# Three chunks of a hybrid layer's q/k/v projection, by seven products of half blocks and ahead of the cache decode instead of beside it

## The chip, the core and the metric

One core of one Trainium2 chip runs the whole kernel. The metric is device time in microseconds (us). Before the change it is 1711.08 us, the median of 3 runs (1709.94 to 1711.53). Engines are named as the profile names them: PE (TensorE, matmuls), PEld (its weight loads), DVE (VectorE), ACT (ScalarE), POOL (GpSimd), SP (SyncE, which issues the DMAs).

## What is computed

One layer over 1024 prompt tokens and 128 sample tokens (8 sequences of 16). Its first part is what matters here: a norm, one projection to q, k and v for two groups of 8 heads, and two kinds of attention. The sample tokens also attend to a cache (1024 past frames in group A, 512 in group B).

```python
h = rmsnorm(x, g_mix)
q_a, k_a, v_a, q_b, k_b, v_b = split_heads(h, w_in)      # h @ w_in, 1024 x 3072
...
def stick_breaking(q, k, v, q_pos, k_pos):               # group A
    z = jnp.einsum('bqhd,bkhd->bhqk', q, k).astype(jnp.float32) * (HEAD_DIM ** -0.5)
    causal = k_pos[None, :] < q_pos[:, None]
    log_keep = jnp.where(causal, jax.nn.log_sigmoid(-z), 0.0)
    between = lax.cumsum(log_keep, axis=3, reverse=True) - log_keep
    w = jnp.where(causal, jnp.exp(jax.nn.log_sigmoid(z) + between), 0.0)
    return jnp.einsum('bhqk,bkhd->bqhd', w.astype(v.dtype), v)
...
x = x + mix @ w_out
h = rmsnorm(x, g_ffn)
x = x + (jax.nn.silu(h @ w_gate) * (h @ w_up)) @ w_down
```

## The kernel before

Tokens lie in nine tiles of 128: tiles 0 to 7 are the prompt, tile 8 (`NP`) the sample tokens. Every fp32 operand of a large product is split into a high part (a cast on ACT) and a low part (a subtraction, `sub`, L104), and `mm3` (L99 to L102) issues three matmuls for each pair: high by high, high by low, low by high.

`qkv` (L227) makes the projection in twelve chunks of 256 columns, named (group, w, c): group 0 is A and 1 is B, w is 0 for queries, 1 for keys, 2 for values, c is the half. It is a generator: each `yield` is one step of the *main* work, and other generators are advanced between its steps.
- A step of `others` (keys and values, L258) is one token tile: 24 matmuls with 256 moving columns. Three tiles on, keys are turned by PE transposes (L273) and stored; values are split and stored.
- A step of `queries` (L244) is one half of the chunk's columns by three token tiles: 24 matmuls with 384 moving columns, then a scaled split (`parts`) and two stores.

`load` brings a chunk's weights (1 MB) and splits them, one chunk ahead; there is one buffer for raw weights and two for split ones.

The order of the main work is the list `loads` (L299): keys of A, queries of A, values of A, keys, values, queries of B. The stage ahead of the decode runs 36 steps of it (L785 to L795): A's keys (18), A's queries (12), and tile 8's share of A's values (6). Then `decode(0, ...)` (L334, group A's sample tokens against the cache) runs beside 30 steps: `advance(project, dec, R2, 30)` (L806) takes R2 = 1.2 decode steps for each main step. PE's order is as written there (`manual_schedule`). A decode step transposes a block of cached keys on PE (L405), copies it out on ACT and DVE (L406), multiplies (L427), takes sigmoids, and for an earlier block turns weights (L414) and multiplies by cached values (L468). Once a sequence DVE scans the kept shares and multiplies them in (`between`, L114, and L444).

Then the attention over the prompt (`attention`, L515, run from L817) takes 1.95 of its units for each remaining main step (values and queries of B, 30 steps). A unit is one head by one tile of 128 queries: two score matmuls for each block of keys (L579, L580), two sigmoids on ACT (L582, L583), the scan on DVE (`between`, L111 and L114), a multiplication on POOL (L592), and five units later (`LAG`) the transposes (L610), their split on ACT and DVE (L614, L105), and the products with the values (L633, L634). A head has 8 units and 36 transposes at L610; group A has 8 heads, so 64 units. Outside `manual_schedule` a scheduler with its own model of durations sets the order on each engine. After group A's heads, group B's heads run beside `decode(1, ...)`.

The feed-forward part already multiplies by seven products of half blocks instead of eight (`product`, L1077; `sums`, L1099).

## Time and profile before

| | |
|---|---|
| median of 3 runs | 1711.08 us |
| profiled execution, its own time | 1711.13 us |
| span of that execution, first to last instruction | 1709.3 us |
| granted clock of TensorE, mean | 0.989 |
| PE, DVE, ACT, POOL busy | 1654.1, 1080.7, 813.3, 832.5 us |
| first instruction of the cache decode (L405) | 151.75 us |
| first scores of the attention (L579) | 333.64 us |

The time of an execution is 1.8 us more than its span. Matmuls overlap: the profile gives one with 256 moving columns as 0.28 us long, but the next one starts 0.12 us later. What one costs in a stream is therefore read from start to start, and "busy" on PE is no measure of free room.

### The profile page before, as it was taken

Reading aid. Unit: us, or ns where it says so; the run is one execution under the profiler, and the core shown is the slowest. Engines: PE = TensorE matmul, PEld = TensorE weight load, DVE = VectorE, ACT = ScalarE, POOL = GpSimd, SP = SyncE. Lnnn points to the kernel's source line nnn. Section 1 sums busy time; section 2 is a strip of 40 time slices with the busy share of each in tenths; the row PEclk is TensorE's granted clock in tenths of the full one; section 3 lists DMA queues with packets and bytes.
Section 4 is the critical chain, followed back from the end, with each engine's and each line's share of the span. In section 5 each row is a group of like instructions: output and inputs, shape, how many; then the busy total and the mean of one; then the engine's idle time right before and its main releaser. Section 6 shows DMA issues by size and latency. Waiting matters only on the chain.

```text
span 1709.3 us, 27802 instructions
## 1 busy us (share of the span) xinstructions
PE 1654.1 (97%) x10308; PEld 1422.4 (83%) x10308; DVE 1080.7 (63%) x1725; ACT 813.3 (48%) x1724; POOL 832.5 (49%) x675
## 2 busy tenths in 40 slices
PE   8999999999998999798999999999999999999998
PEld 7998888989996778787878888888888878788887
DVE  6111444369789766754677566666655497798875
ACT  5323545367768767643663333333333244433673
POOL 2313311278466412222565555555555378958763
PEclk9999999999998999899999999999999999999999
DMA  5846898666469985856422222222222697722222
GB/s 193 276 151 217 268 294 291 185 186 184 114 186 268 278 269 159 244 160 198 144 91 96 96 96 95 96 95 96 87 86 87 226 377 252 248 70 112 98 99 99
DMA packets 172810, 293.50 MB, mean 172 GB/s; under 512 B 16641, under 2 KB 96257, under 8 KB 170370
## 3 DMA queue, kind: packets, MB, share of 16 engines
q1 hardware_dynamic: 172674, 291.71, 52.4%
q8 instruction: 82, 1.34, 0.3%
q14 instruction: 54, 0.44, 0.1%
HBM read 204.77 MB, written 86.90 MB: 171 GB/s over the span
## 4 chain that ended last, share of the span: by engine, by line
PE 76%; DMA 6%; DVE 6%; POOL 4%; ACT 4%; issue 4%; SPq 1%; POOLq 0%; DVEq 0%; ACTq 0%
PE ps L1081 25%; PE ps L100 6%; PE ps L101 6%; PE ps L102 6%; PE pt L1081 4%; PE pt L610 3%; PE pt L405 2%; PE pt L1352 2%; PE ps L1352 2%; PE po L634 2%; PE acc L468 2%; DMA v<-sv 2%; PE po L633 1%; PE sdec L427 1%; PE S L579 1%
## 5 line engine op out<-in xcount | busy, mean ns | idle before, releaser
L105 POOL TENSOR_TENSOR wlo<-wraw,whi 128x512 fp32r<-128x512 f32 (+1 forms) x121 | 217.6, 1821 | 125.2 <-ACT whi L159 121.7
L100 PE MATMUL ps<-whi,hTh 128*128 128x256 f32 x576 | 168.7, 293 | 1.3 <-ACT st L267 1.3
L101 PE MATMUL ps<-wlo,hTh 128*128 128x256 f32 x576 | 164.7, 286 | 0.0
L102 PE MATMUL ps<-whi,hTl 128*128 128x256 f32 x576 | 164.5, 286 | 0.0
L159 ACT CAST whi<-wraw 128x512 fp32r<-128x512 f32 (+1 forms) x118 | 86.2, 746 | 75.5 <-PE ps L1081 27.4
L100 PEld LDWEIGHTS ps<-whi,hTh 128*128 128x128 f32 x576 | 111.3, 193 | 8.0 <-issue 6.0
L101 PEld LDWEIGHTS ps<-wlo,hTh 128*128 128x128 f32 x576 | 111.4, 193 | 0.2
L102 PEld LDWEIGHTS ps<-whi,hTl 128*128 128x128 f32 x576 | 111.1, 193 | 0.6 <-DVE hTl L105 0.2
L592 POOL TENSOR_TENSOR w<-w,keep 128x127 f32<-128x127 f32 (+4 forms) x64 | 82.3, 1291 | 57.1 <-DVE keep L114 35.1
L105 DVE TENSOR_TENSOR wtl<-pt,wth 128x512 fp32r<-128x512 f32 (+1 forms) x192 | 93.9, 511 | 14.9 <-ACT wth L614 14.6
L614 ACT CAST wth<-pt 128x512 fp32r<-128x512 f32 (+1 forms) x192 | 85.6, 468 | 35.5 <-PE pt L610 34.9
L610 PE MATMUL pt<-ident,w 128*128 128x128 f32 x528 | 90.2, 285 | 11.7 <-DVE osb L649 4.1
L114 DVE TENSOR_TENSOR_SCAN keep<-keep,zero 128x128 f32<-128x128 f32 (+7 forms) x64 | 99.4, 1556 | 1.5
L610 PEld LDWEIGHTS pt<-ident,w 128*128 128x128 f32 x528 | 63.9, 144 | 25.1 <-issue 7.0
L579 PE MATMUL S<-qk 128*128 128x384 f32 (+2 forms) x192 | 73.2, 383 | 6.2 <-ACT keep L583 3.8
L633 PE MATMUL po<-wth,vk 128*128 128x256 f32 (+1 forms) x304 | 76.4, 283 | 0.8 <-DMA vk<-v 0.5
L105 POOL TENSOR_TENSOR actl<-actr,acth 128x1024 fp32r<-128x1024 f32 (+1 forms) x22 | 60.5, 2751 | 33.0 <-DMA sr<-acts 20.7
L634 PE MATMUL po<-wtl,vk 128*128 128x256 f32 (+1 forms) x304 | 72.8, 284 | 0.0
L101 PE MATMUL ps<-hTl,whi 128*128 128x384 f32 x192 | 65.6, 342 | 0.0
L406 DVE COPY kT<-pt 128x512 f32<-128x512 f32 x48 | 33.0, 687 | 51.6 <-PE pt L405 47.6
L100 PE MATMUL ps<-hTh,whi 128*128 128x384 f32 x192 | 65.5, 341 | 0.0
L102 PE MATMUL ps<-hTh,wlo 128*128 128x384 f32 x192 | 64.9, 338 | 0.0
(450 smaller groups left out, 5304.8 us busy)
## 6 DMA issues: line engine op xcount, KB each, us to landing
draw<-in_cache_sb_k SPq DMA_DIRECT2D x32, 512.0 KB, 5.7
draw<-in_cache_sb_v SPq DMA_DIRECT2D x32, 512.0 KB, 5.3
act<-sg SPq DMA_DIRECT2D x11, 1152.0 KB
actr<-act SPq DMA_DIRECT2D x22, 576.0 KB, 6.3
wraw<-in_w_in SPq DMA_DIRECT2D x11, 1024.0 KB, 9.3
wraw<-in_w_gate SPq DMA_DIRECT2D x11, 1024.0 KB, 5.4
wraw<-in_w_up SPq DMA_DIRECT2D x11, 1024.0 KB, 5.4
v<-sv SPq DMA_DIRECT2D x36, 256.0 KB, 4.6
```

Of the source, the lines that this page charges most:

```text
L100: T.matmul(out, lhsT=ah, rhs=bh, start=start, stop=False)
L101: T.matmul(out, lhsT=ah, rhs=bl, start=False, stop=False)
L102: T.matmul(out, lhsT=al, rhs=bh, start=False, stop=stop)
L105: return eng.tensor_tensor(out, a, hi.bitcast(F32), op=ALU.subtract)
L114: V.tensor_tensor_scan(rev, rev, zero[:, 0:1].to_broadcast([P, n - d]), keep[:, n - d : n - d + 1], op0=ALU.mult, op1=ALU.max)
L159: A.copy(h[:, o], v[:, o])
L579: T.matmul(sc, lhsT=hd["qq"][:, qs], rhs=hd["kkh"][:, kc], start=True, stop=False)
L610: T.transpose(pt[:, (c - c0) * P : (c - c0 + 1) * P], w[:, c * P : (c + 1) * P], ident)
L614: A.copy(wth[:, ks, qs], pv)
L633: T.matmul(dst, lhsT=vs, rhs=wth[:, kb - base, c0:c1], start=(i == 0), stop=False)
L634: T.matmul(dst, lhsT=vs, rhs=wtl[:, kb - base, c0:c1], start=False, stop=(i == nkb - 1))
L1081: T.matmul(out, lhsT=a[x][:, k], rhs=b[y][:, k], start=(not more and k == 0 and n == 0), stop=(k == 3 and n == 2), skip_group_check=more)
```

## The change

Three of the twelve chunks, A's second query chunk (0, 0, 1) and B's two key chunks (1, 1, 0) and (1, 1, 1), are made by `seven`. The prompt is cut into two halves of four tiles, the 1024 inputs into two halves, the 256 columns into two halves; seven block products of 12 matmuls with 512 moving columns (`product`) take the place of eight. They need sums of blocks: `sum_forms` builds four sums of input blocks once (14 DVE instructions on 128x512 for each of four k, and 4 casts on ACT), beside the steps of the second key chunk and the first query chunk; `weight_sums` builds four of the weights for each chunk (4 DVE instructions, then 4 casts on ACT and 4 subtractions on POOL). Tile 8 is done apart (`sampled`): 48 matmuls with 128 moving columns for the query chunk, 24 with 256 for a key chunk.

The token groups become 4, 4 and 1 tiles, so that a step of `queries` has 512 moving columns, or 128 for tile 8. The order of the main work becomes: A's keys, A's first query chunk, the three chunks by `seven`, tile 8's share of A's values, and only then the decode; the rest of the values goes beside the decode (23 steps, 1.5 decode steps each), and the last six steps of values and all of B's queries beside the attention (2.25 units each). Pools for the sums are opened after the first nine steps and closed just ahead of the decode.

```diff
-        def __init__(self):
+        def __init__(self, ends=(3, 6, 9)):
...
-            g, o = divmod(t, 3)
+            g, o = self.group(t)
...
+    def weight_sums(pool, v):
+
+        (a11, a12), (a21, a22) = [[v[:, k * 4 : k * 4 + 4, f * P : (f + 1) * P] for k in range(2)] for f in range(2)]
+        s1, s2, s3, s4 = [pool.tile([P, 4, P], F32, name=f"s{i}", tag=f"s{i}", bufs=1) for i in (1, 2, 3, 4)]
+        V.tensor_tensor(s1, a21, a22, op=ALU.add)
+        V.tensor_tensor(s2, s1, a11, op=ALU.subtract)
+        V.tensor_tensor(s3, a11, a21, op=ALU.subtract)
+        V.tensor_tensor(s4, a12, s2, op=ALU.subtract)
+        return s1, s2, s3, s4
...
+        def queries(grp, c, wts, gs=(0, 2, 1)):
...
-            order = [(pr, g) for pr in range(2) for g in range(3)]
-            if (grp, c) == (1, 1):
-                order.sort(key=lambda x: x[1])
+            order = [(pr, g) for g in gs for pr in range(2)]
             for pr, g in order:
                 m = slice(pr * P, (pr + 1) * P)
-                ps_ = ps["o"].tile([P, 384], F32, name="ps", tag="O")
+                n = hT.count[g] * P
+                ps_ = ps["o"].tile([P, 512], F32, name="ps", tag="O")[:, :n]
...
+                    if k == 3 and n > 256:
+                        yield
+                cut = min(n, stg[1])
+                cut = 256 if cut == 384 else cut
+                for o in range(0, n, cut):
+                    d = min(cut, n - o)
+                    transposed_out(grp, 0, c * 2 + pr, hT.first[g] * P + o, d, parts(d, ps_[:, o : o + d], (1 - 2 * grp) * HD**-0.5))
                 yield
...
+        def sum_forms():
...
+            for k in range(4):
...
+                yield op(t1, q0h, p0h, minus)
+                yield op(t1, t1, q0l, ALU.add)
+                yield op(t1, t1, p0l, minus)
+                hi("T1", t1)
+                yield op(t2, q1h, t1, minus)
+                yield op(t2, t2, q1l, ALU.add)
+                hi("T2", t2)
+                yield lo("T1", t1)
+                yield op(t4, p1h, t2, minus)
+                yield op(t4, t4, p1l, ALU.add)
+                hi("T4", t4)
+                yield lo("T2", t2)
+                yield op(t3, q1h, q0h, minus)
+                yield op(t3, t3, q1l, ALU.add)
+                yield op(t3, t3, q0l, minus)
+                hi("T3", t3)
+                yield lo("T4", t4)
+                yield lo("T3", t3)
...
+        def sampled(grp, w, c, wts):
...
+                for pr in range(2):
+                    ps_ = ps["o"].tile([P, 512], F32, name="ps", tag="O")[:, :P]
+                    m = slice(pr * P, (pr + 1) * P)
+                    for k in range(KT):
+                        mm3(ps_, wts[0][:, k, m], wts[1][:, k, m], *hT.tok(NP, k), k == 0, k == KT - 1)
+                    transposed_out(grp, 0, c * 2 + pr, NP * P, P, parts(P, ps_, (1 - 2 * grp) * HD**-0.5))
+                return
+            ps_ = ps["o"].tile([P, 256], F32, name="ps", tag="O")
+            for k in range(KT):
+                mm3(ps_, *hT.tok(NP, k), wts[0][:, k], wts[1][:, k], k == 0, k == KT - 1)
+            st = stg[0].tile([P, 3, 256], F32, name="st", tag="st", bufs=2)
+            A.copy(st[:, 0], ps_)
+            rows_of(grp, c, st, NP, 1)
...
+        def seven(grp, w, c, nxt, summed):
+
...
+            S = {1: weight_sum_parts(pool_, 1, s)}
+            B11, B21, B22 = hT.block(0, 0), hT.block(0, 1), hT.block(1, 1)
...
+            a = bank()
+            product(a, quarter(wts, 0, 0), B11)
+            u2 = pool_.tile([P, 512], F32, name="u2", tag="u2", bufs=2)
+            u3 = pool_.tile([P, 512], F32, name="u3", tag="u3", bufs=1)
+            A.copy(u2, a)
...
+            fetch(*nxt)
+            yield
+            product(a, quarter(wts, 1, 0), B21, True)
+            S[3] = weight_sum_parts(pool_, 3, s)
+            yield
+            done(0, 0, a)
+            b = bank()
+            product(b, S[1], F["T2"])
+            V.tensor_tensor(u2, u2, b, op=ALU.add)
+            yield
+            cc = bank()
+            product(cc, S[2], F["T3"])
+            V.tensor_tensor(u3, u2, cc, op=ALU.add)
+            load(*nxt, summed)
+            yield
+            d = bank()
+            product(d, S[0], F["T1"])
+            V.tensor_tensor(u3, u3, d, op=ALU.add)
+            yield
+            sampled(grp, w, c, wts)
+            done(1, 1, u3)
+            yield
+            product(cc, quarter(wts, 1, 1), F["T4"], True)
+            V.tensor_tensor(u3, u2, cc, op=ALU.add)
+            done(1, 0, u3)
+            yield
+            product(d, S[3], B22, True)
+            V.tensor_tensor(u2, u2, d, op=ALU.add)
+            done(0, 1, u2)
+            yield
+
...
+        wide["open"]()
+        sums_ = sum_forms()
+        load(0, 0, 0)
...
+        yield from beside(others(0, 1, 1, ready[0, 1, 1], range(3)))
+        load(0, 0, 1, True)
+        yield from beside(queries(0, 0, ready[0, 0, 0]))
+        for _ in sums_:
+            pass
+        chunks = [(0, 0, 1), (1, 1, 0), (1, 1, 1)]
+        for i, x in enumerate(chunks):
+            after = chunks[i + 1] if i + 1 < len(chunks) else None
+            yield from seven(*x, after or (0, 2, 0), after is not None)
+        fetch(0, 2, 1)
+        load(0, 2, 1)
+        yield from others(0, 2, 0, ready[0, 2, 0], (2,))
+        yield from others(0, 2, 1, ready[0, 2, 1], (2,))
+        wide["close"]()
+        yield from others(0, 2, 1, ready[0, 2, 1], (0, 1))
+        ch.turn = 1 - ch.turn
+        load(1, 2, 0)
+        yield from others(0, 2, 0, ready[0, 2, 0], (0, 1))
+        load(1, 2, 1)
+        yield from others(1, 2, 0, ready[1, 2, 0], range(3))
+        load(1, 0, 0)
+        yield from others(1, 2, 1, ready[1, 2, 1], range(3))
+        load(1, 0, 1)
+        yield from queries(1, 0, ready[1, 0, 0])
+        yield from queries(1, 1, ready[1, 0, 1])
...
+        sv = dk.tile([P, 2, 4, 2, HD], F32R, name="sv")
+        odd = dk.tile([P, 2], F32, name="odd")
+        place = dk.tile([P, 528 if grp else 16], F32, name="bias" if grp else "own_place")
+        loaded = {(x, w): dk.tile([P, 4, P], F32, name=f"s{w}{x}", tag=f"s{w}", bufs=1) for w in "qk" for x in (0,)}
         for i in range(ahead):
             fetch(i)
...
-    stg = pool(right, "stg", "right", 2)
+    sstack = ExitStack()
+    stg = [pool(sstack, "stg", "right", 2), 512]
...
+    hT = Transposed((4, 8, 9))
+    for g in (0, 2, 1):
...
+    def open_wide():
+        fp = pool(wstack, "qforms", "left")
+        wide["forms"] = {n: [fp.tile([P, KT // 2, 512], F32R, name=n + x) for x in "hl"] for n in ("T1", "T2", "T4", "T3")}
+        wide["pool"] = pool(wstack, "qsums", "left")
+        wide["banks"] = wstack.enter_context(tc.tile_pool(name="ps_w", bufs=3, space=PSUM, side="right", reuse_waits="tile"))
...
+    def close_wide():
+        wstack.close()
+        sstack.close()
+        stg[:] = pool(right, "stg2", "right", 2), 384
+        wide["closed"] = True
...
-    advance(project, None, 0, 36 - (NT - 1))
+    while "closed" not in wide:
+        next(project)
...
-        advance(project, dec, R2, 30)
+        advance(project, dec, 1.5, 24 - 1)
...
-    advance(project, att, 1.95)
+    advance(project, att, 2.25)
```

Counted over PE's whole order, the matmuls of the projection stand so (transposes: those of keys):

| stage on PE | 256 wide | 384 wide | 512 wide | 128 wide | transposes |
|---|---|---|---|---|---|
| before: up to the first L405 | 624 | 288 | 0 | 0 | 36 |
| before: from there to the first scores | 799 | 0 | 0 | 0 | 36 |
| before: from there on | 305 | 288 | 0 | 0 | 0 |
| after: up to the decode's first transpose | 696 | 0 | 348 | 96 | 56 |
| after: from there to the first scores | 648 | 0 | 9 | 0 | 0 |
| after: from there on | 0 | 0 | 183 | 96 | 0 |

The first place is on PE ahead of the decode, where A's second query chunk is made; `hTh_140` holds the second half of the inputs of the first tiles, `whi` and `wlo` are the weights. Before it reads:

```order
L100 MATMUL ps<-hTh_140,whi 128x384
L101 MATMUL ps<-hTl_141,whi 128x384
L102 MATMUL ps<-hTh_140,wlo 128x384
L100 MATMUL ps<-hTh_140,whi 128x384
L101 MATMUL ps<-hTl_141,whi 128x384
```

With the change, `T3` and `T1` being sums of inputs and `S2` and `S0` sums of weights:

```order
L216 MATMUL ps<-hTh_140,whi 128x512
L216 MATMUL ps<-hTl_141,whi 128x512
L216 MATMUL ps<-hTh_140,wlo 128x512
L216 MATMUL ps<-T3l,S2h 128x512
L216 MATMUL ps<-T3h,S2l 128x512
L216 MATMUL ps<-T1h,S0h 128x512
L216 MATMUL ps<-T1l,S0h 128x512
```

The products are wider, and some of them read tiles that DVE, ACT and POOL have just made. The second place is on DVE in the same stage. Before, it holds the splits of the keys (`sq<-pt`) and of the queries (`sq<-ps`), and copies of values:

```order
L105 TENSOR_TENSOR sq<-pt,sq 128x384 x4
L267 COPY st<-ps 128x256
L105 TENSOR_TENSOR sq<-pt,sq 128x384 x2
L237 SCALAR_TENSOR_TENSOR sq<-ps,sq 128x384 x12
L267 COPY st<-ps 128x256 x3
```

With the change (L368 are sums of inputs in scratch tiles `tS..`, L228 to L231 sums of weights):

```order
L105 TENSOR_TENSOR T2l<-tS3l,T2h 128x512
L368 TENSOR_TENSOR tS0l<-tS0l,hTl_149 128x512
L368 TENSOR_TENSOR tS0h<-tS0h,hTl_141 128x512
L368 TENSOR_TENSOR tS3h<-tS3h,hTl_139 128x512
L368 TENSOR_TENSOR tS0l<-tS0l,hTl_147 128x512
L368 TENSOR_TENSOR tS3l<-hTh_148,tS3h 128x512
L105 TENSOR_TENSOR T4l<-tS0h,T4h 128x512
L105 TENSOR_TENSOR T1l<-tS3h,T1h 128x512
```

Between two splits of keys or queries now stand up to fourteen instructions with two inputs in SBUF. The third place is on PE in the attention, in the fifth head, which before has main matmuls (L100 to L102) between its own:

```order
L634 MATMUL po<-wtl,vk 128x256
L633 MATMUL po<-wth,vk 128x128
L634 MATMUL po<-wtl,vk 128x128
L610 MATMUL pt<-ident,w 128x128 x4
L100 MATMUL ps<-hTh_142,whi 128x384
L579 MATMUL S<-qk 128x384
L580 MATMUL S<-qk 128x384
L101 MATMUL ps<-hTl_143,whi 128x384
```

With the change (L771 and L772 are the scores, L802 the transposes, L825 and L826 the products with values):

```order
L802 MATMUL pt<-ident,w 128x128 x4
L771 MATMUL S<-qk 128x512
L772 MATMUL S<-qk 128x512
L802 MATMUL pt<-ident,w 128x128
L771 MATMUL S<-qk 128x384
L772 MATMUL S<-qk 128x384
L771 MATMUL S<-qk 128x512
L772 MATMUL S<-qk 128x512
L802 MATMUL pt<-ident,w 128x128 x6
```

From the fourth head's end on, no main matmul stands in PE's order: the main matmuls between the last transposes of successive heads were 185, 98, 80, 75, 78, 75, 2 and 0 before, and are 105, 67, 81, 26, 0, 0, 0 and 0 now.

171 lines of the change are left out of this document (100 added, 71 removed).

## The prediction

> **What bounds the kernel now.** I read the page first, then a table of windows by stage, then PE's timeline for start-to-start times, then the chain of waits and the costliest groups of single stages. The page says that PE is busy nearly all the time:
>
> ```profile
> span 1709.3 us, 27802 instructions
> PE   8999999999998999798999999999999999999998
> DVE  6111444369789766754677566666655497798875
> ```
>
> That is not yet a bound, since overlapping matmuls count in full. The windows below are cut at the first cache transpose (151.75), the first scores (333.64), and then at the last transpose of each head of group A's attention (each 36th at L610):
>
> ```profile
> core 0: us, PE busy (x) PEld busy (x) DVE busy (x) ACT busy (x) POOL busy (x), PEclk, DMA share, GB/s
> 50.00:151.75 101.75, 100.46 (x711) 100.22 (x710) 12.95 (x25) 25.04 (x50) 26.67 (x17) 1.00 0.62 205
> 151.75:333.64 181.89, 178.85 (x1998) 158.29 (x1996) 74.43 (x120) 83.14 (x218) 35.84 (x42) 0.99 0.80 257
> 333.64:372.55 38.91, 35.77 (x264) 33.75 (x265) 21.73 (x28) 21.93 (x57) 26.30 (x31) 0.96 0.80 225
> 372.55:400.09 27.54, 26.53 (x209) 25.23 (x208) 24.72 (x35) 20.20 (x55) 20.88 (x24) 1.00 0.55 156
> 400.09:427.33 27.24, 26.84 (x191) 25.65 (x190) 25.34 (x36) 19.98 (x49) 23.76 (x25) 1.00 0.60 185
> 427.33:454.13 26.80, 26.80 (x186) 26.07 (x184) 22.94 (x38) 19.09 (x46) 15.45 (x20) 1.00 0.51 141
> 454.13:481.59 27.46, 27.46 (x189) 26.66 (x188) 22.28 (x35) 19.10 (x46) 14.11 (x18) 1.00 0.47 137
> 481.59:508.38 26.79, 26.79 (x185) 26.02 (x184) 21.46 (x34) 17.54 (x45) 14.03 (x19) 1.00 0.52 151
> 508.38:530.91 22.53, 17.46 (x110) 14.22 (x109) 21.71 (x30) 17.61 (x45) 15.33 (x21) 0.87 0.99 297
> 530.91:563.06 32.15, 28.65 (x248) 22.94 (x247) 29.70 (x59) 28.20 (x72) 21.50 (x25) 0.93 0.92 255
> ```
>
> Three stages, three states. Ahead of the decode (first row) PE is full and DVE nearly idle, 13 of 102 us. Beside the decode PE is full and the DMA is at 0.80. In the attention the middle heads have PE full with DVE at 80% and more; the seventh head (508 to 531), beside which no main matmul is left, takes 22.53 us, and there DVE is the full one: 21.71 us. So a head costs about 22.5 us by DVE, whatever PE has to do, and main work beside it is free up to the difference.
>
> What a matmul costs from start to start, by width:
>
> ```profile
> 28.07 0.28 PE L102 MATMUL ps<-whi,hTl 128*128 128x256 f32 x1
> 28.19 0.28 PE L100 MATMUL ps<-whi,hTh 128*128 128x256 f32 x1
> ...
> 103.96 0.34 PE L101 MATMUL ps<-hTl,whi 128*128 128x384 f32 x1
> 104.13 0.33 PE L102 MATMUL ps<-hTh,wlo 128*128 128x384 f32 x1
> ...
> 902.20 0.39 PE L1081 MATMUL ps<-B21h,whi 128*128 128x512 f32 x1
> 902.43 0.39 PE L1081 MATMUL ps<-B21l,whi 128*128 128x512 f32 x1
> ...
> 362.26 0.28 PE L579 MATMUL S<-qk 128*128 128x128 f32 x1
> 362.37 0.27 PE L580 MATMUL S<-qk 128*128 128x128 f32 x1
> 362.48 0.27 PE L634 MATMUL po<-wtl,vk 128*128 128x128 f32 x1
> ```
>
> So 256 columns cost 0.120 us, 384 cost 0.173, 512 cost 0.227, and 128 cost 0.11: nearly as much as 256, where 0.06 would be in proportion. From the chain of waits, in the decode:
>
> ```profile
> 200.10 0.31 PE ps L100
> 203.16 0.87 PE pt L405 x8
> 205.48 1.02 PE pt L405 x8
> 207.75 0.32 PE ps L100
> ```
>
> Eight transposes take 0.87 us, 0.109 each.
>
> **Ahead of the decode.** By the counts of the table in the section on the change, this stage gains 348 matmuls of 512 (79.0 us), 96 of 128 (10.6), 72 of 256 (8.6) and 20 transposes (2.2), and loses 288 of 384 (49.8): +50.6 us. The seventh product saved in each chunk is in it: 12 matmuls, 2.7 us, three times, 8.2 us; the narrow matmuls of tile 8 eat most of that (at 0.06 each they would cost 4.8 us less; the rows of 0.11 are the only ones of such matmuls in succession, so I take those). PE is full here, so this stands on the path one for one. Nothing can come back below it: PE's idle time in the window is 1.3 us.
>
> Beside it DVE gets 56 instructions for the sums of inputs and 12 for those of the weights, and POOL 12 subtractions. The nearest rows are those of the same sums in the feed-forward part:
>
> ```profile
> L1103 DVE TENSOR_TENSOR s<-wraw 128x512 f32<-128x512 f32 x22 | 26.4, 1200 | 3.8 <-DMA wraw<-in_w_gate 3.8
> L1105 DVE TENSOR_TENSOR s<-wraw 128x512 f32<-128x512 f32 x22 | 15.2, 692 | 17.0 <-POOL S2l L105 11.1 <-DMA wraw<-in_w_up 3.7 <-DMA wraw<-in_w_gate 1.8
> L105 POOL TENSOR_TENSOR wlo<-wraw,whi 128x512 fp32r<-128x512 f32 x86 | 132.8, 1572 | 12.9 <-ACT whi L159 10.9 <-ACT whi L988 2.0
> ```
>
> One shape, one kind, 692 or 1200 ns. At 692 the 56 are 39 us, at 1200 they are 67. The steps they lie beside are nine of keys (9x24x0.120 = 26 us) and the first query chunk (96x0.227 + 48x0.11 = 27 us), and the splits of keys and queries need DVE too (some 8 us). So it fits at 692 (47 in 53 us) and not at 1200 (75). The sums have until their products come, another 8 to 20 us on, but PE's order has some of those products early. POOL is quieter here than in the feed-forward part (27 of 102 us), so I stay near the lower end: 4 us of waiting, bounds 0 and 12. The Trainium skill ("SBUF — State Buffer", section "Who interferes with whom") says that a VectorE instruction with two inputs in SBUF locks out GpSimd's reads, and the reverse, for a whole instruction; all 56 are of that kind, and the two prices of one shape agree with it. By it each overlap costs a whole instruction of the other engine, which is the upper bound above.
>
> **The decode.** Here go 151 matmuls of 256 (18.1 us) and 36 transposes of keys (3.9); 9 of 512 come (2.0): -20.0 us. The pace before, by the groups and the window of 200 to 301.9 us:
>
> ```profile
> L100 PE MATMUL ps<-whi,hTh 128*128 128x256 f32 x136 | 40.1, 295 | 0.0
> ...
> 200.00:301.90 101.90, 101.90 (x1210) 90.43 (x1206) 47.13 (x79) 50.81 (x137) 16.22 (x21) 1.00 0.89 292
> ```
>
> 136 at L100 are 17 blocks of main work in 101.9 us, 5.99 us each with 1.2 decode steps: 2.88 for the block, so 2.6 for a decode step, and two steps in a row take 2.3 each (205.48 less 203.16, 207.75 less 205.48, rows above). PE's idle time there is none; what is taken away shortens it. Two things can take some back. First, DMA: at 292 GB/s and 5.0 us a step moves 1.46 MB, of which 1.05 are two blocks of cache; with 1.5 steps to a block that is 1.38 MB in (2.88 + 1.5x2.6)/1.5 = 4.5 us, 306 GB/s, while the seventh head above shows 297 GB/s at a share of 0.99. If 297 is the ceiling, a step takes 4.65, some 4 us over the stage. Second, every fourth step DVE holds the copies of keys back (a scan, a multiplication, and only then the copy that PE's next transposes wait for):
>
> ```profile
> 169.37 2.36 DVE keep L114
> 171.75 3.22 DVE wdec L444
> 174.98 0.61 DVE kT L406
> 175.63 1.09 PE pt L405 x8
> ```
>
> Between two decode steps without a block PE has 2.3 us of work to cover that; such pairs are one in five steps now and one in two then. I take 4 us for both together, bounds 0 and 8. -16.0.
>
> **The attention.** A middle head holds 75 main matmuls of 384 (13.0 us) in 26.80, so its own work on PE is 13.8. By the counts, main work beside the heads becomes 18.2, 15.2, 12.8, 5.9, 0, 0, 0 us, where it was 22.2, 11.8, 12.7, 13.0, 13.5, 13.0, 0.3. Head by head: the first 38.9 - 4.0 = 34.9; the second 13.8 + 15.2 and half a us, 29.5; the third 13.8 + 12.8, 27.0 with the like; the fourth has 19.7 on PE and falls to DVE's 22.5; the fifth, sixth and seventh stay at 22.5. Sum 181.4, where the seven took 197.3: -15.9. What leaves the attention is 34 us of main work; what comes back is 16, because from the fourth head on DVE ends last. Bounds: DVE's 20.5 (1 us under the least of its rows, 21.46) gives -24, 24.5 a head gives -8. The eighth head has the group B decode beside it before and after, and the rest of the program stands in the same order.
>
> **Sum.** +50.6 + 4 - 16.0 - 15.9 = +22.7 us on the profiled execution's 1711.13 (span 1709.3 and 1.8 around it), which is the median's 1711.08 within 0.1: 1734 us.
>
> **The rivals.**
> - *Faster: the attention keeps TensorE's pace.* If the heads without main work run at PE's 13.8 us rather than DVE's 22.5 (the fourth at 19.7), the attention gives back 44.8, and without the two waits the sum is 50.6 - 20.0 - 44.8 = -14: 1697. It turns where the four take 18.8 us a head. For it: the seventh head had the DMA at 0.99, so DVE need not be all that held it. Against: DVE is busy 21.5 to 25.3 us in every head. 5%.
> - *DVE becomes the bound ahead of the decode.* With the sums at 1200 ns, 28 us more on DVE, of which PE waits for perhaps 20 in place of my 4: 1750. It decides from about 0.9 us an instruction. For it: the 1200. Against: POOL's 27 of 102 us. 9%.
> - *The decode keeps its pace of 5.0 us a step,* since the cache cannot come faster. 34 steps times 0.5 us, 17, in place of my 4: 1747. For it: 0.89 at 292 GB/s. Against: 297 and 306 lie close, and there are bytes less. 12%.
> - *TensorE's clock falls in the heads without main work.* The seventh head shows a granted clock of 0.87. At that clock 13.8 us are 15.9, still under 22.5, so it costs nothing; at half they would be 27.6, 5 us over in each of four heads, +20: 1754. 2%. The Trainium skill ("TensorE: Matmul & The Clock Gate", section "What's actually happening") has the clock at half after an idle window of about 3.4 us; the 0.87 says that here this holds for a small part of the time.
>
> **How the numbers follow.** The forecast has 72%. Its own range: with all lower bounds, 45.8 + 0 - 20 - 24 = +2; with all upper, 50.6 + 12 - 12 - 8 = +43. Ends seldom come together, so +10 to +38. The rivals above reach from 1747 to 1754, the faster one to 1697. Leaving out the faster one and a few per cent at each end gives 1720 to 1750. Some 0.2% (3.4 us) is what a measurement can tell from no change: faster by more 5%, within it 3%, slower by more 92%.
>
> **What would show it.** In the profile after: the decode's first transpose near 151.75 + 55 = 206 us; the first scores near 372; the fifth to seventh heads 22 to 23 us each with DVE busy over 21 and PE's sum of starts far below; from the eighth head on the same durations as before, 23 us later. Wrong would be: a first transpose after 220 (then DVE's sums), a decode pace above 4.8 us a step (DMA or the scans), or heads without main work well under 21 us.

## The result, and the profile after

The changed kernel takes **1755.57 us** (median of 4 runs, 1754.85 to 1756.48); the kernel before took 1711.03 on the same chip (4 runs, 1709.94 to 1711.53). The ratio is 1.026, 95% interval 1.0244 to 1.0279: slower, as forecast, but by 44.5 us and not by 23. The time lies 5.6 us above the range.

The profiled execution, cut at the places that the prediction used (us; a gain of the change is negative):

| stage | before | after | difference | forecast |
|---|---|---|---|---|
| start to the decode's first cache transpose | 151.75 | 220.63 | +68.9 | +54.6 |
| from there to the first scores | 181.89 | 163.82 | -18.1 | -16.0 |
| seven heads of group A's attention | 197.3 | 192.5 | -4.8 | -15.9 |
| all that follows | 1178.4 | 1176.2 | -2.2 | 0 |
| span | 1709.3 | 1753.1 | +43.8 | +22.7 |

Two terms failed, 14 us ahead of the decode and 11 us in the attention. The table of windows of after, one row for each of the seven heads (each ends with its 36th transpose, now L802):

```profile
core 0: us, PE busy (x) PEld busy (x) DVE busy (x) ACT busy (x) POOL busy (x), PEclk, DMA share, GB/s
384.45:422.42 37.97, 32.34 (x186) 27.13 (x185) 24.50 (x35) 18.22 (x50) 14.39 (x23) 0.91 0.75 203
422.42:451.66 29.24, 29.24 (x177) 25.42 (x176) 23.54 (x38) 20.40 (x50) 14.70 (x20) 1.00 0.45 118
451.66:478.66 27.00, 27.00 (x193) 24.76 (x192) 22.67 (x37) 18.08 (x47) 14.99 (x19) 1.00 0.50 137
478.66:503.00 24.34, 21.87 (x135) 19.16 (x133) 20.30 (x31) 17.57 (x46) 12.07 (x20) 0.93 0.64 175
503.00:530.36 27.36, 18.17 (x111) 15.09 (x109) 26.22 (x36) 20.28 (x51) 19.18 (x24) 0.88 0.89 260
530.36:554.17 23.81, 19.17 (x109) 16.20 (x109) 22.09 (x32) 16.41 (x42) 14.51 (x19) 0.79 0.37 91
554.17:576.91 22.74, 17.12 (x109) 14.16 (x109) 21.65 (x32) 16.70 (x42) 14.59 (x19) 0.88 0.44 115
```

The second, third and seventh heads came out as forecast (29.5, 27.0, 22.5). The first is 3.1 us longer than forecast, the fourth 1.8, the fifth 4.9, the sixth 1.3. The fifth has no main work and yet takes 27.36, with DVE busy 26.22.

Ahead of the decode the waits of PE tell most (what waited, for whom: us, times, longest):

```profile
PE ps L100 <- ACT st L317: 8.0, 3, 6.5
PE ps L102 <- DVE hTl L105: 4.5, 1, 4.5
```

The windows around the longest two waits (columns as in the table above) show that each is paid twice:

```profile
46.00:50.80 4.80, 0.34 (x3) 0.13 (x2) 4.80 (x5) 0.00 (x0) 3.06 (x2) 0.87 0.14 46
50.80:55.00 4.20, 4.13 (x19) 4.14 (x20) 4.20 (x9) 1.24 (x2) 0.00 (x0) 0.50 0.37 89
55.00:60.00 5.00, 5.00 (x39) 5.00 (x38) 4.25 (x8) 1.69 (x5) 0.00 (x0) 0.86 0.64 217
...
208.00:216.00 8.00, 1.54 (x11) 1.33 (x11) 0.42 (x1) 2.15 (x7) 3.76 (x5) 0.84 0.71 245
216.00:220.60 4.60, 4.60 (x24) 4.60 (x24) 0.00 (x0) 0.71 (x2) 1.84 (x3) 0.54 0.64 206
```

In the rows that begin at 46 and 208 us PE starts next to nothing. In those that follow it is full, but at a granted clock of 0.50 and 0.54: 19 matmuls of 256 in 4.2 us, where 0.120 each would make 2.3. The 0.86 of the row from 55 to 60 us says that the half clock reached some 1.4 us into it. By PE's starts, a wait of 4.7 us costs 2.5 more behind it, and that of 6.6 us at 215.65 costs 2.1 more. The Trainium skill ("TensorE: Matmul & The Clock Gate", section "What's actually happening") lets the clock fall to half after an idle window of about 3.4 us and rise again after a busy one of the same length. These two waits agree with the first half of that. The half clock lasted longer behind them, about 5.6 and 4.2 us of these rows, and the runs below have it behind waits of only 2.2 us, shorter than that window; there the measurement decides.

What PE waited for at 46 us, in DVE's timeline (start, duration):

```profile
43.36 0.68 DVE L368 TENSOR_TENSOR tS3h<-hTh,hTh 128x512 f32<-128x512 f32 x1
43.96 2.90 DVE L368 TENSOR_TENSOR tS0l<-hTh,hTh 128x512 f32<-128x512 f32 x1
46.78 2.82 DVE L368 TENSOR_TENSOR tS3h<-tS3h,hTl 128x512 f32<-128x512 f32 x1
49.53 0.68 DVE L368 TENSOR_TENSOR tS0l<-tS0l,hTl 128x512 f32<-128x512 f32 x1
50.13 1.28 DVE L105 TENSOR_TENSOR hTl<-pt,hTh 128x512 fp32r<-128x512 f32 x2
```

and in POOL's:

```profile
43.51 5.55 POOL L105 TENSOR_TENSOR wlo<-wraw,whi 128x1024 fp32r<-128x1024 f32 x2 [3.51 <-ACT whi L159]
```

Four sums of inputs stand ahead of the split of tile 8 (hTl), and the two that run beside POOL's two subtractions take 2.90 and 2.82 us where their like takes 0.68.

What PE waited for at 197 and 215 us is a chain of transfers; the chain of waits for 195 to 222 us begins so:

```profile
189.94 9.13 DMA draw<-in_cache_sb_k
199.14 7.82 DMA v<-sv
...
208.02 5.13 DMA v<-sv
...
215.21 2.03 DMA v<-sv
```

The first blocks of the cache (draw) are fetched here, together with the values' stores (v<-sv), which hold the two staging buffers, and so ACT, and so PE's accumulators. Before, the first of these blocks was asked for at 44.8 us; now at 189.2, because their memory is held by the sums until the seventh product of the last chunk. The run with the move alone (below), which has no sums, asks for the first block at 45.4 us again, and in it PE has no wait for the staging.

### The profile page after: what moved, and what is told of

Read it like the earlier page. It is cut to its first block, busy times and chain, and to the rows that moved or that the text cites. A ratio compares the mean times of both kernels' runs of the same rounds, so it can differ in the third digit from the quotient of the medians.

```text
span 1753.1 us, 27540 instructions
## 1 busy us (share of the span) xinstructions
PE 1668.3 (95%) x10064; PEld 1406.2 (80%) x10064; DVE 1144.3 (65%) x1810; ACT 831.5 (47%) x1763; POOL 849.9 (48%) x693
## 4 chain that ended last, share of the span: by engine, by line
PE 72%; DMA 7%; DVE 5%; ACT 3%; POOL 3%; issue 2%; SPq 1%; POOLq 0%; ACTq 0%; DVEq 0%
PE ps L216 27%; PE ps L100 4%; PE ps L101 4%; PE ps L102 4%; PE pt L1536 4%; PE pt L216 3%; PE ps L1536 3%; PE pt L802 2%; DMA v<-sv 2%; PE pt L597 2%; DVE keep L114 1%; PE po L826 1%; PE po L825 1%; PE acc L660 1%; PE S L771 1%
## 5 line engine op out<-in xcount | busy, mean ns | idle before, releaser
L100 PE MATMUL ps<-whi,hTh 128*128 128x256 f32 x448 | 133.8, 299 | 8.1 <-ACT st L317 8.0
L102 PE MATMUL ps<-whi,hTl 128*128 128x256 f32 x448 | 130.2, 291 | 4.5 <-DVE hTl L105 4.5
L101 PE MATMUL ps<-wlo,hTh 128*128 128x256 f32 x448 | 129.8, 290 | 0.0
L784 POOL TENSOR_TENSOR w<-w,keep 128x127 f32<-128x127 f32 (+4 forms) x64 | 78.2, 1224 | 76.7 <-DVE keep L114 51.1
L802 PE MATMUL pt<-ident,w 128*128 128x128 f32 x528 | 91.3, 293 | 20.5 <-POOL w L784 8.5
L100 PEld LDWEIGHTS ps<-whi,hTh 128*128 128x128 f32 x448 | 88.9, 199 | 14.8 <-ACT st L317 8.6
L802 PEld LDWEIGHTS pt<-ident,w 128*128 128x128 f32 x528 | 65.8, 148 | 35.7 <-POOL w L784 11.4
L102 PEld LDWEIGHTS ps<-whi,hTl 128*128 128x128 f32 x448 | 88.8, 198 | 5.1 <-DVE hTl L105 5.0
L771 PE MATMUL S<-qk 128*128 128x384 f32 (+2 forms) x192 | 76.3, 400 | 14.6 <-ACT keep L775 11.5
L101 PEld LDWEIGHTS ps<-wlo,hTh 128*128 128x128 f32 x448 | 89.0, 199 | 0.4 <-issue 0.2
L825 PE MATMUL po<-wth,vk 128*128 128x256 f32 (+1 forms) x304 | 79.3, 292 | 0.4 <-DVE wtl L105 0.2
L826 PE MATMUL po<-wtl,vk 128*128 128x256 f32 (+1 forms) x304 | 74.2, 288 | 0.0
L105 POOL TENSOR_TENSOR S3l<-s,S3h 128x512 fp32r<-128x512 f32 x24 | 32.4, 1350 | 76.0 <-ACT S3h L236 67.9
L105 POOL TENSOR_TENSOR S2l<-s,S2h 128x512 fp32r<-128x512 f32 x24 | 35.3, 1469 | 64.8 <-PE ps L216 35.4
L105 POOL TENSOR_TENSOR sv<-st,sv 128x256 fp32r<-128x256 f32 x36 | 26.3, 734 | 79.3 <-ACT sv L326 69.5
```

The costliest lines, as they stand in the source:

```text
L100: T.matmul(out, lhsT=ah, rhs=bh, start=start, stop=False)
L101: T.matmul(out, lhsT=ah, rhs=bl, start=False, stop=False)
L102: T.matmul(out, lhsT=al, rhs=bh, start=False, stop=stop)
L105: return eng.tensor_tensor(out, a, hi.bitcast(F32), op=ALU.subtract)
L771: T.matmul(sc, lhsT=hd["qq"][:, qs], rhs=hd["kkh"][:, kc], start=True, stop=False)
L802: T.transpose(pt[:, (c - c0) * P : (c - c0 + 1) * P], w[:, c * P : (c + 1) * P], ident)
```

## The experiments

Times below are medians beside runs of the kernel before on the same chip (1710 to 1711); the changed kernel is 1755.57. Stages are read from each run's profiled execution.

### The first theory: two waits ahead of the decode

**The sums held until the split.** Every sum of inputs is kept on DVE until tile 8's split has been issued:

```
             A.copy(dh, pv)
-            sub(V, dl, pv, dh)
+            splits[:] = [sub(V, dl, pv, dh)]
...
-                    V.tensor_tensor(out, a, b, op=o)
+                    with tc.issue_after(splits[-1].ins):
+                        V.tensor_tensor(out, a, b, op=o)
```

> The changed kernel, with the first of the sums of inputs held on DVE until the split of tile 8 has been issued (before, two of them of 2.9 and 2.8 us stood ahead of it, and PE waited 4.5 us for that split at 46 us). Theory A (order on DVE): that wait goes and what follows has slack, so 4 to 5 us less, 1751. Theory B (DVE simply has too much to do up to 110 us, where PE's windows show some 5 us more of waiting): the wait comes back a few steps later, 0 to 1.5 us less, 1754 to 1756.

1756.49 us, ratio 1.027 (1.0253 to 1.0286): no gain. The wait for the split is gone, but the first cache transpose comes only 1.7 us earlier (218.96). Theory B holds. Windows of this run:

```profile
46.00:50.80 4.80, 4.17 (x35) 3.94 (x35) 4.80 (x7) 0.37 (x1) 2.19 (x1) 1.00 0.14 48
50.80:55.00 4.20, 4.20 (x37) 4.20 (x36) 4.20 (x8) 2.94 (x6) 0.00 (x0) 1.00 0.97 292
55.00:60.00 5.00, 4.76 (x40) 4.52 (x39) 5.00 (x10) 2.89 (x4) 2.69 (x1) 1.00 0.55 195
60.00:65.00 5.00, 5.00 (x44) 5.00 (x44) 5.00 (x3) 0.33 (x1) 4.09 (x2) 1.00 0.23 79
65.00:70.00 5.00, 4.04 (x34) 3.84 (x33) 5.00 (x10) 2.46 (x6) 0.00 (x0) 1.00 0.97 322
70.00:75.00 5.00, 2.70 (x14) 2.46 (x13) 5.00 (x9) 0.89 (x2) 1.61 (x1) 0.74 0.31 106
```

DVE is busy in every microsecond from 46 to 75 (in the row of 60 to 65 with three instructions), and PE waits again at 66.9 and 72.6 us, 1.1 and 2.5 us, then at a clock of 0.74. Both times it waits for ACT's copy out of an accumulator (st), which stands in ACT's order behind casts that wait for DVE's sums:

```profile
71.62 0.62 ACT L238 CAST S2h<-s 128x512 fp32r<-128x512 f32 x1 [2.39 <-DVE s L232]
72.14 0.37 ACT L319 COPY st<-ps 128x256 f32<-128x256 f32 x1
```

The wait was the first sign of a full DVE; with it gone, the next instruction that needs DVE is late.

**The cache first.** The memory of the sums is given back ahead of the values of tiles 6 to 8, and the decode's first six blocks are asked for there:

```
+        wide["close"]()
+        yield
         yield from others(0, 2, 0, ready[0, 2, 0], (2,))
         yield from others(0, 2, 1, ready[0, 2, 1], (2,))
-        wide["close"]()
...
     dec = decode(0, Chunks(dp, "d", 1024, RAWS, 2), dp)
+    next(dec)
+    advance(project, None, 0, 6)
```

> The changed kernel, with the memory of the sums given back right after the seventh product of the third chunk, so that the first six cache blocks are asked for ahead of the two value steps for tiles 6 to 8 and not among their stores. Theory A (the cache's 3 MB collide with the values' stores): PE's waits of 7.5 us for the value step's staging between 195 and 215 us go, and the first cache transpose comes 6 to 10 us earlier: 1746 to 1750. Theory B (the DMA is full there with the stores of keys too, and the blocks only move the jam some us ahead): 0 to 3 us, 1753 to 1756.

1747.02 us, 1.0215 (1.02 to 1.0229): 8.5 less than the changed kernel. But the gain isn't where theory A put it: the first cache transpose is 1.6 us earlier (219.06), and PE waits for the staging still, now behind the store of the transposed keys (out<-kr), which came among the same blocks:

```profile
PE ps L100 <- ACT st L317: 9.4, 2, 8.8
```

By stages this execution is 6.3 us shorter than the changed kernel's: 1.6 ahead of the decode, 5.6 in the decode (158.18 in place of 163.82), 6.4 longer in the seven heads (198.9), and 5.5 shorter behind them. What moved the heads and the rest was not traced. The decode's part can be placed. The windows of its start, after first:

```profile
220.63:250.00 29.37, 25.49 (x215) 21.14 (x213) 9.02 (x12) 15.31 (x37) 9.90 (x9) 0.94 0.70 221
```

and this run:

```profile
219.06:250.00 30.94, 29.90 (x300) 24.81 (x299) 12.53 (x18) 18.52 (x46) 10.85 (x11) 1.00 0.76 250
250.00:300.00 50.00, 49.35 (x612) 42.58 (x610) 22.85 (x37) 26.55 (x76) 13.42 (x19) 1.00 1.00 340
```

In after PE starts 215 matmuls in the first 29 us of the decode, here 300 in 31. The late cache isn't what costs the decode these 5.6 us: the run with the move alone asks for its first block at 45.4 us, and its decode takes 163.74 us all the same, with 223 starts in the first 29 us. In both, 23 us into the decode, PE waits for a small copy that stands in POOL's order behind a weight subtraction (after: PE's waits, and POOL's timeline):

```profile
PE pt L606 <- POOL wn L648: 2.2, 1, 2.2
240.14 3.11 POOL L105 TENSOR_TENSOR wlo<-wraw,whi 128x1024 fp32r<-128x1024 f32 x1 [3.68 <-ACT whi L159]
243.20 0.19 POOL L648 COPY wn<-wdec 128x16 f32<-128x16 f32 x1
```

Then some 3.4 us follow at half clock (the 0.94 of after's row). The wait and the half clock are 3.5 of the 5.6 us. In the run with the cache first the copy (238.74 us) stands ahead of the subtractions (242.90), and neither the wait nor the half clock is there. Why POOL's order differs isn't shown.

### Is it the seven products, or the move?

**The move alone.** No sums and no seven products; the same chunks stand ahead of the decode in plain matmuls:

```
-        wide["open"]()
-        sums_ = sum_forms()
...
-            yield from seven(*x, after or (0, 2, 0), after is not None)
+            load(*(after or (0, 2, 0)))
+            yield from queries(0, 1, ready[x]) if i == 0 else others(*x, ready[x], range(3))
```

> The changed kernel without its seven products and sums: group A's second query chunk and group B's keys stand at the same place ahead of the decode, but in plain matmuls; decode and attention as in the changed kernel. PE has by counts 384 matmuls of 256 and 16 transposes more and 156 of 512 less, +12.4 us. Theory A (the 18 us of waiting ahead of the decode belong to the sums and to the memory that they hold): +12.4 - 16 = about 4 us less than the changed kernel, 1750 to 1754, and the first cache transpose at 215 to 218. Theory B (they belong to the move itself, its stores and DMA): 12 us more, 1766 to 1770.

1754.94 us, 1.026 (1.0241 to 1.0278), first cache transpose at 222.77. It has 12.4 us more of matmuls than the changed kernel and the same time. PE's starts ahead of the decode add up to 9.9 us beyond the widths' prices, where the changed kernel has 20.3 and the kernel before 2.1. So the seven products save 12 us on PE and lose 10 in waits that their sums and their memory bring. That is theory A for 10.4 of the 18 us only: the first transpose is above its 215 to 218, because the move by itself keeps 7.8. Of its 9.9 us, 9.0 are one wait of 2.2 us for DVE's split of queries, and the half clock behind it, from 91.6 to 105.3 us:

```profile
100.00:105.30 5.30, 5.30 (x16) 4.43 (x17) 0.29 (x1) 0.28 (x1) 0.00 (x0) 0.50 0.09 25
```

Why the clock stayed at half so long, with PE full, isn't shown. And the heads are within 1 us the changed kernel's (192.2 us for the seven, 192.5 there; 28.0 and 22.8 for the fifth and sixth), so what happens in the attention has nothing to do with the products.

**The keys back.** The other half of the change alone: group A's second query chunk by seven products, group B's keys beside the decode as before:

```
-        chunks = [(0, 0, 1), (1, 1, 0), (1, 1, 1)]
+        chunks = [(0, 0, 1)]
...
-        load(1, 2, 0)
+        load(1, 1, 0)
         yield from others(0, 2, 0, ready[0, 2, 0], (0, 1))
+        load(1, 1, 1)
+        yield from others(1, 1, 0, ready[1, 1, 0], range(3))
+        load(1, 2, 0)
+        yield from others(1, 1, 1, ready[1, 1, 1], range(3))
...
-        advance(project, dec, 1.5, 24 - 1)
+        advance(project, dec, R2, 30)
...
-    advance(project, att, 2.25)
+    advance(project, att, 1.54)
```

> The move undone for group B's keys: they stand beside the decode again, in plain matmuls, with before's ratio of 1.2 over 30 steps; ahead of the decode only group A's second query chunk is made by seven products, with all its sums. PE has by counts 5.9 us more than the kernel before. Theory A (what costs is that the keys leave stages that had time for them): +5.9, some 5 of waiting for the sums and 8 to 10 for the late cache: 1727 to 1733. Theory B (what costs are the sums and seven products themselves): nearly all of the 44 us stays, 1745 to 1755.

1730.28 us, 1.0109 (1.0088 to 1.0131): theory A. Of the 44.5 us, 25.3 go with the keys. The other 19 stay with one chunk: against the kernel before, 18.1 ahead of the decode, 5.5 in it (187.43 us) and 3.6 in the seven heads, less 7.7 behind them. The sums of inputs cost the same for one chunk as for three (the wait of 4.69 us for the split is there), and the cache is late here too: its first block is asked for at 140.8 us, and PE waits 5.4 us for the staging ahead of the decode, and in the decode's first step 2.4 for ACT, which waits for a store of values.

### The attention

**Main work spread.** PE's order in the attention is fixed as written, a main step after every 2.2 steps:

```
-    advance(project, att, 2.25)
+    advance(project, att, 0, 2)
+    with tc.manual_schedule(engines={mybir.EngineType.PE}):
+        advance(project, att, 2.2)
```

> The changed kernel, with PE's order in group A's attention fixed as it is written (a main step after every 2.2 steps of attention) in place of the scheduler's, which puts all main work into the first four heads. Theory A (a head costs DVE's 22 to 24 us, and main work is free up to that): the seven heads take 165 to 175 us where they took 192.5, so 1735 to 1740. Theory B (a head of 24 to 27 us is what DVE, POOL and the transfers need whatever PE does, or the fixed order makes PE wait for each step's latency): 0 to 5 us less or some us more, 1750 to 1765.

1758.78 us, 1.0286 (1.0272 to 1.03), 3 more than the changed kernel; its seven heads take 203.4 us, 10.9 more, and what follows them 8.2 less. Theory A falls. Windows of its third to sixth heads:

```profile
455.10:481.30 26.20, 25.33 (x159) 22.26 (x157) 23.80 (x37) 19.05 (x47) 13.48 (x19) 1.00 0.45 121
481.30:508.50 27.20, 24.84 (x147) 21.04 (x145) 21.81 (x34) 17.36 (x46) 11.82 (x18) 0.94 0.45 117
508.50:536.80 28.30, 25.73 (x182) 22.99 (x181) 24.06 (x38) 17.87 (x47) 13.79 (x19) 1.00 0.44 121
536.80:559.90 23.10, 22.39 (x144) 19.63 (x143) 20.53 (x32) 17.61 (x46) 12.33 (x21) 1.00 0.64 160
```

At the widths' prices PE has 24.7, 22.0, 24.4 and 21.7 us of matmuls in these heads, and DVE 20.5 to 24.1 of its own. They take 26.2, 27.2, 28.3 and 23.1: 1.4 to 5.2 us over the larger of the two. In this order main work beside a head isn't free up to DVE's time. Whether another order would make it so is open, since the run fixes PE's order too, and the largest sum of PE's waits in its heads two to seven is for DVE's split of the weights (wtl, 5.9 us in seven waits).

**Half of the scan left out.** In `scores`, `between(keep, ident)` is replaced by its second scan alone.

> The changed kernel, with the scan over each row block's own 128 keys left out in group A's attention, so that DVE has some 4 us less in each head (16 scans of 494 ns in the sixth and seventh) and PE, ACT and POOL have the same. Theory A (DVE's busy time sets a head beside which no main work is left): the fifth to seventh heads are 3 to 4 us shorter each, the fourth 1 to 2, the second and third stay at 29 and 27; 1742 to 1746. Theory B (a head is a chain through ACT, DVE, POOL and PE, or PE at its half clock, and DVE's sum doesn't set it): under 1 us a head, 1752 to 1756.

1753.38 us, 1.0243 (1.0225 to 1.0261), with the sixth and seventh heads at 23.1 and 24.1: theory B. DVE's 3 us less bring nothing. Windows of these two:

```profile
526.80:549.90 23.10, 16.71 (x108) 14.31 (x107) 18.99 (x24) 16.04 (x41) 16.61 (x19) 0.87 0.37 92
549.90:574.00 24.10, 17.50 (x110) 15.04 (x109) 19.10 (x24) 16.45 (x42) 16.77 (x19) 0.85 0.41 109
```

PE's waits in its fifth to seventh heads:

```profile
PE S L771 <- ACT keep L775: 11.2, 9, 2.1
PE pt L805 <- POOL w L786: 4.4, 3, 1.9
```

and ACT's:

```profile
ACT keep L775 <- POOL w L787: 3.2, 2, 1.7
```

PE waits for ACT to empty the scores, and ACT waits for POOL's product of an earlier step to free one of three buffers (keep): DVE isn't full any more, POOL's busy time is 2 us higher than in after, and the loop through the engines is no shorter.

**The product left out,** with the whole scan and with half of it: the line `kept.append(G.tensor_tensor(w[:, : n - 1], w[:, : n - 1], keep[:, 1:], op=ALU.mult))` goes, and the flips read `w` as ACT wrote it.

> The changed kernel with the product on POOL alone left out; DVE has all its scans. Theory A (DVE's 21.7 us and the chain of three buffers are both full): the sixth and seventh heads stay above 21 us, as with the half scan alone, 1748 to 1754. Theory B (the chain alone sets the head, DVE is full only because it stands in it): they fall below 21 us, 1738 to 1746.

> The run with the half scan (no scan over a row block's own 128 keys in group A's attention, DVE 19 us a head) and, besides, the product of weights and scan on POOL left out (16 of 128 to 1023 columns in two heads, some 9 us a head). Theory A (behind DVE stands the chain sigmoid on ACT, scan on DVE, product on POOL in three buffers, which held the half scan's run at 23 to 24 us): with both shorter the sixth and seventh heads fall to 18 to 20 us, the whole to 1738 to 1745. Theory B (the limit behind DVE is elsewhere: PE's half clock, the order of the steps or the score banks): they stay at 22 to 24 us, 1750 to 1754.

1737.71 us (1.0158, 1.0139 to 1.0177) and 1732.11 (1.0131, 1.0109 to 1.0153). Without the product, with all of DVE's scans, the sixth and seventh heads take 18.0 and 19.0 us. That is theory B of the first: the chain that goes through the product set the head. But DVE's busy time fell too, and it is full again at the lower value:

```profile
515.90:533.90 18.00, 14.12 (x99) 11.49 (x97) 17.89 (x29) 15.38 (x39) 4.89 (x12) 1.00 0.68 164
533.90:552.90 19.00, 15.38 (x110) 13.05 (x109) 18.93 (x32) 16.22 (x43) 3.65 (x10) 1.00 0.51 132
```

The reason stands in the groups of the two heads, the longest scan (busy us, mean ns) in after:

```profile
L114 DVE TENSOR_TENSOR_SCAN keep<-keep,zero 128x896 f32<-128x896 f32 x2 | 6.9, 3442 | 0.1
```

and in this run:

```profile
L114 DVE TENSOR_TENSOR_SCAN keep<-keep,zero 128x896 f32<-128x896 f32 x2 | 4.2, 2076 | 0.0
```

In the seventh head, with 32 instructions on DVE in both, its 21.65 us became 18.93: 2.7 us were time that its instructions took longer beside POOL. With half the scan out as well, the answer is mixed: the seventh head takes 17.26 us with DVE at 16.26, but the sixth 21.1 with DVE at 16.7, and the whole lies 6 us under theory A's range. One thing these two runs don't separate: without the product the flips read what ACT wrote, so they no longer wait for DVE's scan either. The runs show that the chain from scan to product to flip holds the head, not which link of it.

**Group B's set-up later.** In the changed kernel the sums of group B's decode set-up (queries, values, keys) stand on POOL in the fifth head:

```profile
511.95 1.28 POOL L560 TENSOR_TENSOR sq<-sq,sq 128x512 f32<-128x512 f32 x1
516.75 1.27 POOL L566 TENSOR_TENSOR nv<-sv 128x512 f32<-128x512 f32 x1
523.71 2.98 POOL L560 TENSOR_TENSOR sk<-sk,sk 128x512 f32<-128x512 f32 x1
```

```
-    next(dec)
+    with tc.issue_after(kept[-1].ins):
+        next(dec)
     advance(att, dec, 0, 3)
```

> The changed kernel, with the set-up of group B's decode (two sums of 128x512 on POOL, the last of its small loads) held until the last head of group A's attention; its first cache blocks stay where they were. Theory A (the fifth head took 27.4 us and not 22.5 because POOL's two sums stand between the attention's steps): the fifth head falls to 23 to 24 us, 1752 or, if the eighth gives nothing back, 1751. Theory B (the fifth head is long because of the cache blocks that land in it, DMA at 0.89): it stays at 27, 1755.

1752.94 us, 1.0244 (1.0221 to 1.0267). The interval overlaps the changed kernel's, so the whole time says little; the profile is plain. The fifth head of this run:

```profile
502.50:526.80 24.30, 17.85 (x110) 14.53 (x108) 23.59 (x35) 18.88 (x46) 13.99 (x21) 0.87 0.99 285
```

24.3 us in place of 27.36, with the cache blocks still in it (DMA at 0.99). Theory A, though just above its 23 to 24: POOL's sums, all three of which moved, and not the transfers. The seven heads together are 1.9 us shorter.

### Is there a better version?

**Three repairs.** The sums after the split; the memory given back early, with SP in written order and one block of cache asked for between two value steps; and tile 8's queries with the tokens as the stationary side:

```
+    with tc.manual_schedule(engines={mybir.EngineType.SP}):
+        next(dec)
+        advance(project, dec, 0.5, 6)
...
-                    for k in range(KT):
-                        mm3(ps_, wts[0][:, k, m], wts[1][:, k, m], *hT.tok(NP, k), k == 0, k == KT - 1)
+            for k in range(KT):
+                mm3(ps_, *hT.tok(t, k), wts[0][:, k], wts[1][:, k], k == 0, k == KT - 1)
```

> The changed kernel with three repairs: the sums held until tile 8's split, the memory given back after the last product and the first cache blocks asked for one by one between the value steps' stores (SP in written order there), and tile 8's queries made with the tokens as the stationary side (24 matmuls of 256 and 2 transposes where 48 of 128 stood). Theory A (the waits at 46 and 195 to 215 us, and the half clock behind them, are what the first transpose came late by): 8 us as in the run with the cache first, some 9 more for the wait that it kept, 1.5 for the sums, and 4 to 8 for the 8.7 us of matmuls: 1728 to 1734, first cache transpose at 202 to 206. Theory B (a wait that is removed comes again at the next buffer): 1740 to 1747, first transpose after 212.

1734.62 us, 1.013 (1.0113 to 1.0148), 21 less than the changed kernel. The first cache transpose is at 208.74, between the two theories: 11.9 us earlier, of which the narrower matmuls are 4.4 by counts. The decode gains 2.9, the seven heads lose 2.8, and 7.9 come from behind the seventh head, where nothing was edited. So the time alone lies just above theory A's range, and the stages speak for a mixture.

**The repairs with the keys back.**

> Group B's keys beside the decode again, as in the run with the keys back, with the three repairs (sums after tile 8's split, cache blocks one by one from an earlier moment, tile 8's queries with tokens stationary), and 1.62 attention steps to a main step. PE has by counts 2.8 us less than the kernel before. Theory A (what the run with the keys back lost are the wait for the split and the late cache): -2.8 and some 5 to 9 of waits that stay, 1711 to 1719. Theory B (the repairs move the waits): 1722 to 1730. Below 1708 it would beat the kernel before, for which nothing speaks but the counts.

1732.14 us, 1.0126 (1.0107 to 1.0146): not better than the keys back alone, and above the ranges of both theories. The first scores come 9.4 us earlier than there (347.85 against 357.28), but the heads take 2.3 us more and what follows them 7.8. That last part, from the seventh head's end to the program's, is 1178.4 us in before, 1176.2 in after, 1168.3 with the repairs, 1170.7 with the keys back and 1178.4 here; the run with the cache first has 1170.6, the one with the sums after the split 1179.6. It moves by some 10 us though no edit touched its steps; what in it moves was not traced, and stays open. So a gain of a few us in the whole time of one of these runs says less than the stage that the edit was made in. No version tried beats the kernel before.

## Why the prediction was wrong, point by point

**Ahead of the decode, the count: right.** PE's starts in after, beyond the widths' prices, add up to 20.3 us, against 2.1 before; the difference, 18.2, and the counted 50.6 make 68.8 of the 68.9. The 0.11 for a narrow matmul held (median 0.11).

**Ahead of the decode, "4 us of waiting, bounds 0 and 12": the step that failed first.** It was 18, above its own upper bound. Three things were missing from it. The sums were weighed as a total of time against a total of cover, but the order puts four of them ahead of a split for which PE waits at once. DVE is full from 46 to 75 us in the run without that wait, so its removal brought 1.7 us. That is the rival "DVE becomes the bound ahead of the decode", which had 9%. All the waits together came near its 20 us, but what DVE brought at 46 us, the 4.7 and the 2.5 behind it, is two fifths of them. The prediction's own sign, "a first transpose after 220 (then DVE's sums)", came true by 0.6 us and named the smaller part. Second, the term had no line for memory: the sums hold what the cache's first blocks went into, and these moved from 44.8 to 189 us, into the values' stores. That is a moved transfer, and the diff shows it (pools opened and closed around the chunks); it cost PE 7.5 us of waits for the staging from 185 to 222 us, and 2.1 at half clock. The run without the sums, with its first block at 45.4 us, has neither. Third, a wait was priced at its length, and these two cost over 2 us more each at half clock.

**The decode, -16.0: right in size (-18.1), with two errors that cancel.** The 4 us set aside for a ceiling of the DMA and for scans weren't needed: in the run with the cache first the stage gains 23.7 us, and moves 340 GB/s from 250 to 300 us, so the 297 of the seventh head was no ceiling. What took 5.6 back in the changed kernel wasn't foreseen: in the main the wait for POOL's copy behind a weight subtraction, and the half clock after it. That the forecast came so near is in part luck. The rival "keeps its pace of 5.0 us" falls.

**The attention, -15.9: the second step that failed, by 11 us.** Heads two, three, six and seven came within 1.3 us. The fourth, which still has 26 main matmuls, is 1.8 over. The fifth, 4.9 over, has group B's set-up on POOL, 3 us by the run that moved it: main work ended earlier, so what follows it started earlier, and the prediction had left it in the eighth head. The first, 3.1 over, holds ACT for 10 us behind a store of values, and PE then waits 4.6 us for ACT; but ACT waited there in the kernel before as well (7.7 us for values, 6.5 for keys), and no run took the difference apart. After, then before:

```profile
ACT sv L326 <- DMA v<-sv: 10.0, 1, 10.0
ACT sv L280 <- DMA v<-sv: 7.7, 2, 4.1
```

The reason given, "from the fourth head on DVE ends last", had the right number for the wrong cause. DVE was busy 21.65 us, but 2.7 of these were POOL's doing, taking DVE's work away brought nothing, and taking POOL's product away, and with it the flips' wait for the scan, brought 4 to 6 us a head. And "main work beside it is free up to the difference" did not hold in the spread run. The rival "the attention keeps TensorE's pace" falls: the heads without main work took 22.7 to 27.4 us.

**The clock.** The rival that the clock falls in heads without main work was right in the sign: 0.79 to 0.88 in the rows. What that costs in these heads no run isolates; where the product is left out the clock is 1.00, and the heads are as long as DVE is busy. Its price showed ahead of the decode, where it wasn't looked for.

**What the change bought.** Moving the keys costs 25 us by the keys-back run: against it the changed kernel has 50.8 us more ahead of the decode, where PE is full, and gets back only 23.6 in the decode and 8.5 in heads that hardly shrink (5.5 more come behind them). The seven products earn 12.4 us by counts and lose nearly all of it to their own waits.

## What to carry to other kernels

Before work is moved out of a stage, ask of that stage whether it would be shorter without it: a head whose loop runs through three engines stays as long as the loop, and busy time of an engine in it may be another engine's doing. When a change opens pools, list what stood in that memory, and when its first transfer started. Price a wait of PE of 2 us or more with the half clock behind it, and don't hold a total of work against a total of cover: look at which instruction the order puts ahead of the one that is waited for.

## What the runs showed of the hardware

- One DVE instruction on 128x512 with two inputs took 0.68 us alone and 2.90 and 2.82 beside two POOL subtractions of 128x1024; the scan of 128x896 took 3442 ns beside POOL's products and 2076 without. The Trainium skill ("SBUF — State Buffer", section "Who interferes with whom") has the two engines exclude each other on a shared port; the rows agree. The prediction had cited it, taken its cost as the upper bound, and stayed near the lower end.
- After 4.7 and 6.6 us without matmuls PE ran at a granted clock of 0.50 and 0.54 over the next 4.2 and 4.6 us. Waits of 2.2 us were followed by half clock too: for 3.4 us in the decode of the changed kernel, for 13.7 in the move-alone run.
- The DMA queues moved 297 GB/s at a share of 0.99 in one head before, and 340 at 1.00 over 50 us in the decode of the run with the cache first: a full share did not stand for one rate.
